# Tokens as the stationary side of the last product, and the last norm taken by partition

## The chip, the cores and the metric

One core of a Trainium2 chip runs the whole program. The metric is device time in microseconds (us), from the start of the program to its end. Engines are named as in the profile: PE is TensorE's matmuls and PEld its weight loads, DVE is VectorE, ACT is ScalarE, POOL is GpSimd, SP is SyncE, whose queue issues the loads of the weights.

## The reference, cut to what matters

```python
def rmsnorm(x, g):
    return x * lax.rsqrt(jnp.mean(x * x, axis=-1, keepdims=True) + EPS) * g

def swiglu(x, w_in, w_out):
    gate, up = jnp.split(x @ w_in, 2, axis=-1)
    return (jax.nn.silu(gate) * up) @ w_out

# h: (1, 512 tokens, 1024), D_FF = 2816, fp32
for i in range(2):                      # mixer A in layer 0, mixer B in layer 1
    h = h + 0.5 * swiglu(rmsnorm(h, norm_g[i, 0]), ffn_w_in[i, 0], ffn_w_out[i, 0])
    h = h + mixer(rmsnorm(h, norm_g[i, 1]))
    h = h + 0.5 * swiglu(rmsnorm(h, norm_g[i, 2]), ffn_w_in[i, 1], ffn_w_out[i, 1])
return rmsnorm(h, final_g)
```

The change concerns the end of the last line of the loop for i = 1 (the product with `ffn_w_out[1, 1]`) and the final `rmsnorm`.

## The kernel before

The residual h stays in SBUF as eight tiles `H[j]`, 128 features on the partitions by 512 tokens. Each fp32 factor is split into a high and a low part (`whi`, `wlo` for weights, `xh`, `xl` or `yh`, `yl` for activations) and a product is three matmuls in a row, L356 to L358: high by high, weights' high by low, weights' low by high. The weight block is the stationary side, the tokens move through the array.

`WeightStream` is the road of the weights. SP loads them in pieces of 128 by 1024 (`raw`, ring of 4 buffers), ACT copies a piece to `whi` (L173), DVE forms `wlo` (L176). A converted piece is a unit. Units of kind P hold eight 128 by 128 blocks; units of kind F are the seven forms of a two-level product with sums of weights (`two_pairs`), which runs the gate and up projections. Converted units live in a ring "w" of 3 pairs and, for F units alone, a ring "x" of 2 pairs. `PLAN` is the fixed order of all units. All engines run their instructions in the order in which the program issues them.

`ffn` ends in three chunks (`CHUNKS`): so many calls of `two_pairs`, which fill tiles `Y` with the gated activations, and then a product of these with the rows of `w_out`, added to H. In the last chunk of the last `ffn` the contraction is over 6 blocks of 128 (`n_k` = 6). Before the change this last product is run in two halves of 256 tokens (`parts` = 2), each with its own 6 units (the last `"P" * 6` of `PLAN` loads and converts the same weights again): first four output blocks side by side (`group`), then four one by one (`single`). After each output block DVE multiplies the bank by the token scale and adds it to H (L629, L630), ACT squares it (L306) and weighs it by the final gain (L1100), DVE adds up the squares (L307). At the end of a half, `norm_scale` sums the squares over the partitions by matmuls with a column of ones (L1109), takes a reciprocal root by Newton steps on DVE (`rsqrt`, L282 to L287), and `norm_rest` spreads the result over the partitions by a matmul (L1120) and multiplies all eight tiles by it: the first half's on POOL (L1128), during the second half's product, the second half's on DVE and POOL (L1126, L1128). The output is stored feature by token and turned on the host.

Of the kernel before, what the change touches and what calls it, by code (L numbers as in the profile page):

```python
# [12 lines left out]
F32 = mybir.dt.float32  # L13
# [6 lines left out]
P = 128  # L20
# [29 lines left out]
PLAN = FFN_PLAN + "P" * 37 + FFN_PLAN + FFN_PLAN + "P" * 72 + FFN_PLAN + "P" * 6  # L50
# [5 lines left out]
class WeightStream:  # L56
# [8 lines left out]
    def __init__(self, nc, pool, dram):  # L65
# [21 lines left out]
        self.lo_engine = nc.vector  # L87

# [142 lines left out]
def tile_trunk(ctx: ExitStack, tc, specs_out, xT, wst, gT, rel, onehot, bu, bv, lng, lnb, wspT, bsp, out):  # L231
# [167 lines left out]
    def ffn(layer, which, norm, finish, begin=None, hooks=None, parts=1, aside=None, mids={}):  # L399
# [10 lines left out]
        with tc.tile_pool(name=uname("ffn"), bufs=1) as fp:  # L410
# [17 lines left out]
            def temp(name):  # L428
                return fp.tile([P, S], F32, tag=name, bufs=1, name=uname(name))
# [163 lines left out]
            for ci, dps in enumerate(CHUNKS):  # L593
# [6 lines left out]
                for i in range(dps):  # L600
# [15 lines left out]

                end = ci == len(CHUNKS) - 1
                if end:
                    W.spool = None
                n = S // (parts if end else 1)  # L620
                for at in range(0, S, n):
                    s = slice(at, at + n)

                    def y_parts(k):
                        return Y[k // 2][0][:, k % 2, s], Y[k // 2][1][:, k % 2, s]

                    def add(j, ps):
                        t = gate_tile()[:, 0]
                        nc.vector.tensor_tensor(t[:, s], ps[:, s], R["h"][:, s], op=ALU.mult)  # L629
                        nc.vector.tensor_tensor(H[j][:, s], H[j][:, s], t[:, s], op=ALU.add)  # L630
                        if end:
                            finish(j, s)

                    first = [bank(tag0) for _ in range(4)]
                    group([ps[:, s] for ps in first], range(4), n_k, spec_out, y_parts,
                          hooks=mids if at else {})
                    for j in range(4):
                        add(j, first[j])
                    for j in range(4, KD):
                        ps = bank(tag1)  # L640
                        single(ps[:, s], j, n_k, spec_out, y_parts)
                        add(j, ps)
# [419 lines left out]
    def into(norm):  # L1062
        return lambda j, s: prepare(j, norm)
# [25 lines left out]
    parts = 2  # L1089
    nt = NT // parts  # L1090
    sq = []

    def finish(j, s):
        if j < KD - 1:
            square(j, s)
        else:
            if not sq:
                sq.append(small.tile([P, S], F32, tag="s1_512", bufs=1, name="last_sq"))
            nc.scalar.activation(sq[0][:, s], H[j][:, s], AF.Square)
        nc.scalar.activation(H[j][:, s], H[j][:, s], AF.Copy, scale=g_sb[:, 6, j:j + 1])  # L1100

    R = {}

    def norm_scale(s, end):
        sums = [bank("aux" if end else "acc") for _ in range(nt)]
        for part in (acc[0], sq[0]):
            for t in range(nt):
                at = s.start + t * P
                mm(sums[t][:, :1], part[:, at:at + P], ones[:, :1], start=part is not sq[0], stop=part is sq[0])  # L1109
        v = small.tile([P, nt], F32, tag="v", bufs=1, name=uname("v"))  # L1110
        for t in range(nt):
            nc.vector.tensor_scalar(v[:, t:t + 1], sums[t][:, :1], 1.0 / D, EPS, op0=ALU.mult, op1=ALU.add)
        R["c"] = rsqrt(v, [P, nt])

    def norm_rest(s, end):
        rc = R["c"]
        ps = bank("aux" if end else "acc")
        for t in range(nt):
            at = s.start + t * P
            mm(ps[:, at:at + P], rc[:, t:t + 1].broadcast_to([P, P]), ident, start=True, stop=True)  # L1120
        rb = small.tile([P, S], F32, tag="nwy512", bufs=1, name=uname("last_rb"))
        nc.scalar.activation(rb[:, s], ps[:, s], AF.Copy)
        for j in range(KD):
            o = H[j][:, s]
            if end and j not in (0, 3, 6):
                nc.vector.tensor_tensor(o, o, ps[:, s], op=ALU.mult)  # L1126
            else:
                nc.gpsimd.tensor_tensor(o, o, rb[:, s], op=ALU.mult)  # L1128
            queue = nc.gpsimd if not end else nc.sync if j % 2 else nc.scalar
# [58 lines left out]
```

## Time and profile before

| What | Value |
|---|---|
| Median of 3 runs | 2132.21 us (2132.17 to 2132.26) |
| Profiled execution, its own time | 2135.96 us |
| Its span (first to last instruction) | 2134.2 us |
| PE busy | 2089.1 us, 98% of the span |
| First matmul of the last product | starts at 2068.76 us |
| Last matmul of the last product | starts at 2120.83 us |

The span is 1.8 us shorter than the execution that it comes from. The profiled execution took 3.7 us more than the median of the timed runs, under 0.2%. Places in the program are given in us from the start of the span.

### The profile page before, as it was taken

The numbers are of one execution on the slowest core, as the hardware profiler recorded it, in microseconds if no ns is written. First come the engines' busy times: TensorE is split into PE (matmuls) and PEld (weight loads), VectorE is DVE, ScalarE is ACT, GpSimd is POOL, SyncE is SP. The second block draws the span as 40 slices with busy tenths as digits, with TensorE's granted clock in tenths as the row PEclk, the third lists the DMA queues.
The fourth block names the chain that finished last, engine by engine and source line by source line (L and its number), as shares of the span: only waits on it lengthen the run. The fifth ranks groups of instructions, "written<-read, shape, count | busy, mean of one in ns | idle before, by whom it ended". The sixth has DMA issues, their size and how long they took to land.

```text
span 2134.2 us, 29989 instructions
## 1 busy us (share of the span) xinstructions
PE 2089.1 (98%) x12344; PEld 1854.3 (87%) x12344; DVE 1500.7 (70%) x2052; ACT 899.3 (42%) x1163; POOL 91.2 (4%) x76
## 2 busy tenths in 40 slices
PE   8999999999999999999999999999999999999996
PEld 6989898788788899997989898788888888999895
DVE  6868687696758686776868686645845567687676
ACT  5535344334445344344535344333323245344353
POOL 0000000243200000000000000000000000000002
PEclk9999999999999999999999999999999999999997
DMA  4233332232122323222232322332232222223232
GB/s 170 96 115 112 105 125 82 89 104 85 60 89 89 119 96 102 100 99 79 99 107 97 113 90 95 134 100 88 84 101 92 82 97 99 99 99 102 96 118 70
DMA packets 59992, 212.34 MB, mean 99 GB/s; under 512 B 6904, under 2 KB 7992, under 8 KB 59728
## 3 DMA queue, kind: packets, MB, share of 16 engines
q1 hardware_dynamic: 56448, 201.35, 27.9%
q0 software_dynamic: 1680, 5.94, 0.8%
q10 hardware_dynamic: 1728, 3.15, 0.4%
q8 instruction: 96, 1.57, 0.3%
q14 instruction: 40, 0.33, 0.0%
HBM read 208.29 MB, written 4.74 MB: 100 GB/s over the span
## 4 chain that ended last, share of the span: by engine, by line
PE 81%; issue 8%; DVE 7%; ACT 3%; DMA 1%; POOL 0%; SPq 0%; POOLq 0%; ACTq 0%; DVEq 0%
PE acc L356 14%; PE acc L357 13%; PE acc L358 13%; PE aux L357 10%; PE aux L356 10%; PE aux L358 10%; DVE wlo L176 1%; ACT whi L173 1%; PE aux L967 1%; PE aux L969 1%; PE aux L968 1%; PE aux L1019 1%; PE acc L967 1%; PE acc L969 1%; PE acc L968 1%
## 5 line engine op out<-in xcount | busy, mean ns | idle before, releaser
L176 DVE TENSOR_TENSOR wlo<-raw,whi 128x1024 fp32r<-128x1024 f32 (+1 forms) x389 | 472.8, 1219 | 317.2 <-ACT whi L173 315.8
L173 ACT ACTIVATE whi<-raw 128x1024 fp32r<-128x1024 f32 (+1 forms) x416 | 433.4, 1050 | 483.1 <-PE acc L357 204.3
L356 PE MATMUL acc<-xh,whi 128*128 128x256 f32 (+1 forms) x888 | 306.6, 345 | 9.3 <-ACT xh L295 6.3
L357 PE MATMUL acc<-xl,whi 128*128 128x256 f32 (+1 forms) x888 | 296.8, 334 | 0.8 <-DVE xl L296 0.8
L358 PE MATMUL acc<-xh,wlo 128*128 128x256 f32 (+1 forms) x888 | 296.6, 334 | 0.0
L356 PEld LDWEIGHTS acc<-xh,whi 128*128 128x128 f32 x888 | 169.9, 191 | 28.3 <-ACT xh L295 6.7
L356 PE MATMUL aux<-xh,whi 128*128 128x256 f32 (+1 forms) x592 | 190.2, 321 | 1.2 <-ACT rh L396 1.2
L358 PE MATMUL aux<-xh,wlo 128*128 128x256 f32 (+1 forms) x592 | 190.0, 321 | 1.3 <-DVE wlo L176 1.3
L357 PE MATMUL aux<-xl,whi 128*128 128x256 f32 (+1 forms) x592 | 189.6, 320 | 0.0
L356 PE MATMUL acc<-th,whi 128*128 128x256 f32 x640 | 182.3, 285 | 6.0 <-ACT u L509 4.5
L357 PEld LDWEIGHTS acc<-xl,whi 128*128 128x128 f32 x888 | 170.0, 191 | 19.0 <-DVE xl L296 1.9
L358 PEld LDWEIGHTS acc<-xh,wlo 128*128 128x128 f32 x888 | 169.7, 191 | 16.9
L357 PE MATMUL acc<-tl,whi 128*128 128x256 f32 x640 | 182.0, 284 | 0.3 <-DVE tl L379 0.3
L358 PE MATMUL acc<-th,wlo 128*128 128x256 f32 x640 | 181.8, 284 | 0.0
L356 PE MATMUL acc<-yh,whi 128*128 128x512 f32 (+1 forms) x376 | 142.7, 379 | 5.1 <-ACT whi L173 5.1
L356 PE MATMUL aux<-th,whi 128*128 128x256 f32 x512 | 144.9, 283 | 0.0
L357 PE MATMUL aux<-tl,whi 128*128 128x256 f32 x512 | 144.9, 283 | 0.0
L358 PE MATMUL aux<-th,wlo 128*128 128x256 f32 x512 | 144.9, 283 | 0.0
L358 PE MATMUL acc<-yh,wlo 128*128 128x512 f32 (+1 forms) x376 | 142.5, 379 | 2.1 <-DVE wlo L176 2.1
L358 PE MATMUL aux<-yh,wlo 128*128 128x512 f32 (+1 forms) x376 | 142.1, 378 | 1.7 <-DVE wlo L176 1.5
L357 PE MATMUL acc<-yl,whi 128*128 128x512 f32 (+1 forms) x376 | 142.3, 379 | 0.0
L356 PE MATMUL aux<-yh,whi 128*128 128x512 f32 (+1 forms) x376 | 142.1, 378 | 0.0
(274 smaller groups left out, 4392.0 us busy)
## 6 DMA issues: line engine op xcount, KB each, us to landing
raw<-in_wst SPq DMA_DIRECT2D x378, 512.0 KB, 3.3
dist<-dist_rows ACTq DMA_DIRECT2D x8, 320.0 KB, 4.1
h<-in_xT SPq DMA_DIRECT2D x8, 256.0 KB, 7.2
tb<-dist POOLq DMA_DIRECT2D x8, 256.0 KB, 3.9
bias<-in_bv POOLq DMA_DIRECT2D x1, 1536.0 KB, 7.4
out<-h POOLq DMA_DIRECT2D x8, 128.0 KB, 2.0
raw<-in_wst SPq DMA_DIRECT2D x2, 256.0 KB, 3.9
wT<-in_wspT POOLq DMA_DIRECT2D x1, 512.0 KB, 8.9
```

The lines of the kernel that those rows point to most:

```text
L173: self.nc.scalar.activation(hi[:, s], src[:, s], AF.Copy)
L176: self.lo_engine.tensor_tensor(lo[:, s], src[:, s], hi[:, s].bitcast(F32), op=ALU.subtract)
L356: mm(ps, wh, xh, start=first, stop=False, **kw)
L357: mm(ps, wh, xl, start=False, stop=False, **kw)
L358: mm(ps, wl, xh, start=False, stop=last, **kw)
L967: mm(banks[t], xh, wh, start=k == 0, stop=False)
L968: mm(banks[t], xl, wh, start=False, stop=False)
L969: mm(banks[t], xh, wl, start=False, stop=k == KD - 1)
L1019: mm(ps[:, t * P:(t + 1) * P], V[t][:, d * P:(d + 1) * P], wT[:, g, :], start=True, stop=True)
```

## The change

The last product runs once, over all six units. The tokens become the stationary side (128 of them for each of four token tiles t) and the weights move, 512 columns (half of the 1024 output features) for each matmul. The result has tokens on the partitions and features along the row.

- `PLAN` loses its last six units; the last six (`LAST`) may use both rings and are all kept until the end. The sixth goes into `W.extra`, the tiles `TH[0]`, `TL[0]`, free once the last form has run.
- `turn_back` transposes the old residual on PE, four 128 by 128 blocks into one PSUM bank, and ACT copies the bank to a tile `final[t]`. There are eight of these: four stand between the forms of the last `two_pairs`, four between the steps k of the last product.
- The product runs over k with four banks open (t = 0, 1, two halves each), then bank by bank for t = 2 and 3, with the same kept weights.
- After a bank, `rest`: DVE multiplies it by the token's scale and adds the residual (one instruction, L1146), ACT squares it and sums along the row (`accum_out`, L1149), DVE multiplies by the gain (L1151), which is now a row, loaded by a DMA that repeats it on 128 partitions. After both halves of a token tile, `store`: `rsqrt` on one column, the scale of one half on ACT (L1163), of the other on DVE (L1161), and a store of 256 KB from each of the two queues ACT and SP.

The sums by matmul, the spreading matmul, POOL's multiplications and the second half's weights are gone.

```diff
-PLAN = FFN_PLAN + "P" * 37 + FFN_PLAN + FFN_PLAN + "P" * 72 + FFN_PLAN + "P" * 6
+PLAN = FFN_PLAN + "P" * 37 + FFN_PLAN + FFN_PLAN + "P" * 72 + FFN_PLAN
+LAST = 2 * CHUNKS[-1]
...
     def _parts(self, u, ring):
+        if ring is None:
+            self.conv[u] = self.extra
+            return self.extra
...
-            rings = [r for r in ("w", "x")[:1 if kind == "P" else 2] if self._free(r, self.current)]
+            kept = u >= len(self.units) - LAST
+            rings = [r for r in ("w", "x")[:1 if kind == "P" and not kept else 2]
+                     if self._free(r, len(self.units) - LAST if kept else self.current)
+                     and self._free(r, self.current)]
+            if kept and not rings and self.extra and u == len(self.units) - 1:
+                rings = [None]
...
+                    if last and n_dp == sum(CHUNKS) - 1:
+                        between = last[0](bank("acc"), gate_tile)
                     two_pairs(pair, "aux" if n_dp % 2 else "acc", between)
...
+                if end and last:
+                    W.extra = [x[0].rearrange("p a b -> p (a b)") for x in (TH, TL)]
+                    last[1](n_k, spec_out, y_parts, R["c"], temp)
+                    continue
...
-    ffn(1, 1, 5, finish, parts=parts, mids={2: lambda: norm_scale(head, False), 5: lambda: norm_rest(head, False)})
-    tail = slice(S - S // parts, S)
-    norm_scale(tail, True)
-    norm_rest(tail, True)
+    def turn_back(t, half):
+        ps = turned[0]
+        for i in range(4):
+            nc.tensor.transpose(ps[:, i * P:(i + 1) * P], H[4 * half + i][:, t * P:(t + 1) * P], ident)
+        if not half:
+            final[t] = W.spool.tile([P, D], F32, tag=("r22", "wsum")[t // 2], bufs=2, name=uname("turned"))
+        nc.scalar.activation(final[t][:, half * 512:(half + 1) * 512], ps, AF.Copy)
...
+        turn = [lambda a=a: turn_back(*a) for a in ((0, 0), (0, 1), (1, 1))]
+        return turn[:2] + [lambda: None] * 2 + [load_gains, turn[2]]
...
+        def product(t, half, ps, k):
+            if k not in weights:
+                weights[k] = W.take(*[spec(k, c) for c in range(KD)])
+            s = slice(half * 512, (half + 1) * 512)
+            wh, wl = (w[:, s] for w in weights[k])
+            yh, yl = y_parts(k, slice(t * P, (t + 1) * P))
+            mm(ps, yh, wh, start=k == 0, stop=False)
+            mm(ps, yl, wh, start=False, stop=False)
+            mm(ps, yh, wl, start=False, stop=k == n_k - 1)
...
+        def rest(t, half, ps):
+            x = final[t][:, half * 512:(half + 1) * 512]
+            nc.vector.scalar_tensor_tensor(x, ps, rh[:, t:t + 1], x, op0=ALU.mult, op1=ALU.add)
+            junk = small.tile([P, S], F32, tag="s0_512", bufs=1, name=uname("junk"))
+            i = 2 * t + half
+            nc.scalar.activation(junk, x, AF.Square, accum_out=sums[:, i:i + 1])
+            y = weighed[t, half] = temp(("m1", "m5", "u2", "u3")[i % 4])
+            nc.vector.tensor_tensor(y, x, gains[half], op=ALU.mult)
+
+        def store(t):
+            v = small.tile([P, 1], F32, tag="v", bufs=1, name=uname("v"))
+            nc.vector.tensor_tensor(v, sums[:, 2 * t:2 * t + 1], sums[:, 2 * t + 1:2 * t + 2], op=ALU.add)
+            nc.vector.tensor_scalar(v, v, 1.0 / D, EPS, op0=ALU.mult, op1=ALU.add)
+            rs = rsqrt(v, [P, 1])
+            for half, queue in ((0, nc.scalar), (1, nc.sync)):
+                y = weighed[t, half]
+                if half:
+                    nc.vector.tensor_scalar(y, y, rs[:, :1], None, op0=ALU.mult)
+                else:
+                    nc.scalar.activation(y, y, AF.Copy, scale=rs[:, :1])
+                queue.dma_start(out[t, :, half * 512:(half + 1) * 512], y)
+
+        group2 = [(t, half, bank("aux")) for t in range(2) for half in range(2)]
+        for k in range(n_k):
+            for t, half, ps in group2:
+                product(t, half, ps, k)
+            if k < 4:
+                turn_back(2 + k // 2, k % 2)
+        for t, half, ps in group2:
+            rest(t, half, ps)
+            if half:
+                store(t)
+        for t in range(2, NT):
+            for half in range(2):
+                ps = bank("acc")
+                for k in range(n_k):
+                    product(t, half, ps, k)
+                rest(t, half, ps)
+            store(t)
```

Three places show how the instructions now stand. The first is PE's queue where the last product begins, behind the last form of `two_pairs`. Before, the moving side stands ahead of the stationary one in a row: `yh`, `yl` move, 256 columns at a time.

```order
L358 MATMUL acc_17999<-th_15217,wlo_18063 128x256
L356 MATMUL aux_18225<-yh_17869,whi_18121 128x256
L357 MATMUL aux_18225<-yl_17870,whi_18121 128x256
L358 MATMUL aux_18225<-yh_17869,wlo_18122 128x256
L356 MATMUL aux_18226<-yh_17869,whi_18121 128x256
```

Now the same place of PE's queue reads as follows (the second to fourth bank's rows, of the same kind, lie between the two pieces):

```order
L1138 MATMUL aux_18259<-whi_18106,yh_17869 128x512
L1139 MATMUL aux_18259<-whi_18106,yl_17870 128x512
L1140 MATMUL aux_18259<-wlo_18107,yh_17869 128x512
...
L1108 MATMUL acc_17999<-ident,h_71 128x128
L1108 MATMUL acc_17999<-ident,h_72 128x128
L1108 MATMUL acc_17999<-ident,h_73 128x128
L1108 MATMUL acc_17999<-ident,h_74 128x128
L1138 MATMUL aux_18259<-whi_18139,yh_17869 128x512
```

The weights move, 512 columns at a time, and each step k uses one unit (`whi_18106`, then `whi_18139`), with four transposes of the residual behind it.

The second place is ACT's queue around the end of the last `two_pairs`: `whi` are conversions of units, L543 and L465 the silu and the high part of the last `Y`. Before:

```order
L173 ACTIVATE whi_18155<-raw_17995 128x1024
L173 ACTIVATE whi_18186<-raw_17997 128x1024
L543 ACTIVATE gate_18002<-gate_18002 128x1024
L465 ACTIVATE yh_18221<-gate_18002 128x1024
L173 ACTIVATE whi_18253<-raw_18033 128x1024
L173 ACTIVATE whi_18283<-raw_18125 128x1024
L303 ACTIVATE sqacc_18316<-h_71 128x256
```

Now (L553 and L475 are the same silu and high part, L1111 the copies of the turned residual):

```order
L183 ACTIVATE whi_18210<-raw_18034 128x1024
L1111 ACTIVATE turned_18184<-acc_17999 128x512
L183 ACTIVATE whi_18245<-raw_18110 128x1024
L553 ACTIVATE gate_18003<-gate_18003 128x1024
L475 ACTIVATE yh_18252<-gate_18003 128x1024
L1111 ACTIVATE turned_18279<-acc_17999 128x512
L183 ACTIVATE th_15214<-raw_18143 128x1024
L1111 ACTIVATE turned_18279<-acc_17999 128x512
L1111 ACTIVATE turned_18316<-acc_17999 128x512 x2
L1149 ACTIVATE junk_18360,last_sums_18258<-turned_18040 128x512
```

The fourth and fifth of the six units (`whi_18210`, `whi_18245`) have moved ahead of the silu, the sixth stands behind it, in `th_15214`, and no conversion is left behind it.

The third place is the end of DVE's queue. Before, after the last Newton step (`nwy`), it multiplies five tiles of the second half:

```order
L287 SCALAR_TENSOR_TENSOR nwy_18737<-nwt_18736,nwy_18737 128x2
L1126 TENSOR_TENSOR h_72<-h_72,aux_18749 128x256
L1126 TENSOR_TENSOR h_73<-h_73,aux_18749 128x256
L1126 TENSOR_TENSOR h_75<-h_75,aux_18749 128x256
L1126 TENSOR_TENSOR h_76<-h_76,aux_18749 128x256
L1126 TENSOR_TENSOR h_78<-h_78,aux_18749 128x256
```

Now this is all that DVE does for a token tile (t = 2), and then the first row of t = 3; the Newton steps between are 11 rows, of which the first and last stand:

```order
L1146 SCALAR_TENSOR_TENSOR turned_18279<-acc_18421,last_rh_18256,turned_18279 128x512
L1151 TENSOR_TENSOR m_1444_18443<-turned_18279,gate_18178 128x512
L1146 SCALAR_TENSOR_TENSOR turned_18279<-acc_18445,last_rh_18256,turned_18279 128x512
L1151 TENSOR_TENSOR m_1447_18467<-turned_18279,gate_18178 128x512
L1155 TENSOR_TENSOR v_18469<-last_sums_18258 128x1
L1156 TENSOR_SCALAR v_18469<-v_18469 128x1
L292 TENSOR_SCALAR nwi_18472<-v_18469 128x1
...
L297 SCALAR_TENSOR_TENSOR nwy_18474<-nwt_18473,nwy_18474 128x1
L1161 TENSOR_SCALAR m_1447_18467<-m_1447_18467,nwy_18474 128x512
L1146 SCALAR_TENSOR_TENSOR turned_18316<-acc_18490,last_rh_18256,turned_18316 128x512
```

The next tile's first instruction stands behind the whole chain of the tile before, on the same queue.

## Rows read from the trace of the kernel before

**Rows 1.** Windows: length, busy PE, PEld, DVE, ACT, POOL, clock, DMA share, GB/s.
```profile
2068.80:2083.60 14.80, 14.58 (x121) 14.37 (x120) 10.40 (x18) 7.99 (x13) 0.00 (x0) 1.00 0.34 108
2083.60:2098.40 14.80, 11.15 (x82) 9.96 (x81) 8.44 (x15) 7.67 (x13) 0.00 (x0) 1.00 0.31 107
2098.40:2109.40 11.00, 10.86 (x78) 10.43 (x77) 9.55 (x24) 4.12 (x9) 4.21 (x7) 0.84 0.07 24
2109.40:2121.30 11.90, 5.93 (x25) 5.27 (x24) 9.49 (x15) 4.93 (x10) 6.63 (x10) 0.61 0.18 66
2121.30:2134.20 12.90, 3.25 (x12) 2.78 (x12) 4.68 (x21) 1.41 (x4) 2.08 (x3) 0.50 0.25 81
```

**Rows 2.** Timeline of PE: start, duration, instruction (first two and last matmul).
```profile
2068.76 0.28 PE L356 MATMUL aux<-yh,whi 128*128 128x256 f32 x1
2068.88 0.28 PE L357 MATMUL aux<-yl,whi 128*128 128x256 f32 x1
...
2120.83 0.41 PE L358 MATMUL acc<-yh,wlo 128*128 128x256 f32 x1
```

**Rows 3.** PE's longest wait from 2068.8 to the end: total us, times, longest.
```profile
PE acc L356 <- ACT whi L173: 5.1, 2, 4.6
```

**Rows 4.** Timeline of DVE: one line while POOL multiplies, and later.
```profile
2105.94 1.19 DVE L307 TENSOR_TENSOR sqacc<-sqacc,sq 128x256 f32<-128x256 f32 x1 [0.48 <-ACT sq L306]
...
2120.89 0.42 DVE L307 TENSOR_TENSOR sqacc<-sqacc,sq 128x256 f32<-128x256 f32 x1 [0.48 <-ACT sq L306]
```

**Rows 5.** Timeline behind the last product: first and last instruction of the Newton steps.
```profile
2123.91 0.17 DVE L282 TENSOR_SCALAR nwi<-v 128x2 int32<-128x2 int32 x1
...
2125.88 0.16 DVE L287 SCALAR_TENSOR_TENSOR nwy<-nwt,nwy 128x2 f32<-128x2 f32 x1
```

**Rows 6.** Timeline of POOL: the two last multiplications.
```profile
2128.58 1.39 POOL L1128 TENSOR_TENSOR h<-h,last_rb 128x256 f32<-128x256 f32 x2
```

**Rows 7.** Timeline of PE, mixer B: weights moving, 512 columns (first and last of 22).
```profile
1360.94 0.39 PE L967 MATMUL aux<-whi,xh 128*128 128x512 f32 x1
...
1365.70 0.39 PE L967 MATMUL aux<-whi,xh 128*128 128x512 f32 x1
```

**Rows 8.** Timeline of PE at the program's start: 512 columns.
```profile
7.55 0.63 PE L356 MATMUL acc<-xh,whi 128*128 128x512 f32 x1
7.98 0.63 PE L357 MATMUL acc<-xl,whi 128*128 128x512 f32 x1
```

**Rows 9.** Timeline of PE in mixer A: four transposes, and the instruction behind them.
```profile
594.47 0.60 PE L874 MATMUL aux<-ident,pr 128*128 128x128 f32 x4
594.91 1.29 PE L886 MATMUL acc<-pT,v 128*128 128x128 f32 x7
```

**Rows 10.** One line's instructions: duration in ns, least, median, most.
```profile
L874 PE MATMUL aux<-ident,pr x80: 270/271/273, 500.8 to 594.8; 128*128 128x128 f32 x80
```

**Rows 11.** Groups by form: count, busy us, mean ns, idle before.
```profile
L984 DVE SCALAR_TENSOR_TENSOR z<-aux,rcol,bias 128x512 f32<-128x512 f32 x12 | 8.9, 739 | 3.9 <-PE aux L969 3.9
L542 DVE TENSOR_TENSOR gate<-gate,u 128x512 f32<-128x512 f32 x36 | 24.6, 685 | 0.0
L997 DVE TENSOR_SCALAR bv<-bv,mv,nwy 128x512 f32<-128x512 f32 x24 | 12.0, 542 | 0.0
L306 ACT ACTIVATE sq<-h 128x512 f32<-128x512 f32 x7 | 4.4, 623 | 3.3 <-DVE sqacc L307 3.3
L860 ACT ACTIVATION_READ_ACCUMULATOR pr<-lg,st 128x1 f32 x32 | 6.0, 187 | 0.0
L436 ACT ACTIVATE m<-h,g_sb 128x512 f32<-128x512 f32 x32 | 21.2, 710 | 0.0
```

**Rows 12.** Groups by form: the conversions of a unit.
```profile
L173 ACT ACTIVATE whi<-raw 128x1024 fp32r<-128x1024 f32 x412 | 431.2, 1054 | 483.1 <-PE acc L357 204.3 <-PE aux L357 138.2 <-issue 45.8
L176 DVE TENSOR_TENSOR wlo<-raw,whi 128x1024 fp32r<-128x1024 f32 x385 | 470.2, 1225 | 317.2 <-ACT whi L173 315.8
```

**Rows 13.** DMA issues: a row of DRAM repeated on 128 partitions, us to landing.
```profile
bias<-in_bv POOLq DMA_DIRECT2D x1, 1536.0 KB, 7.4
```

More of the change, by code (lines that the diff above doesn't have):

```diff
@@ L87, in __init__ @@
         self.lo_engine = nc.vector
+        self.extra = None
     def _free(self, ring, below):
@@ L230, in tile_trunk @@
 @with_exitstack
-def tile_trunk(ctx: ExitStack, tc, specs_out, xT, wst, gT, rel, onehot, bu, bv, lng, lnb, wspT, bsp, out):
+def tile_trunk(ctx: ExitStack, tc, specs_out, xT, wst, gT, gl, rel, onehot, bu, bv, lng, lnb, wspT, bsp, out):
     nc = tc.nc
@@ L397, in scale_rows, with ffn @@
         return rb, rh
-    def ffn(layer, which, norm, finish, begin=None, hooks=None, parts=1, aside=None, mids={}):
+    def ffn(layer, which, norm, finish, begin=None, hooks=None, aside=None, last=None):
         NJ = DFF // P
@@ L426, in ffn, with temp @@
                 begin(spare)
-            def temp(name):
-                return fp.tile([P, S], F32, tag=name, bufs=1, name=uname(name))
+            def temp(name, width=S):
+                return fp.tile([P, width], F32, tag=name, bufs=1, name=uname(name))
             def sums(kp):
@@ L615, in spec_out, with y_parts, add @@
                     return ("ffn_w_out", (layer, which), (p0 + k) * P, [(0, c * P, P)])
+                def y_parts(k, s=slice(0, S)):
+                    return Y[k // 2][0][:, k % 2, s], Y[k // 2][1][:, k % 2, s]
                 end = ci == len(CHUNKS) - 1
+                if end and last:
+                    W.extra = [x[0].rearrange("p a b -> p (a b)") for x in (TH, TL)]
+                    last[1](n_k, spec_out, y_parts, R["c"], temp)
+                    continue
                 if end:
                     W.spool = None
[L620 to L642, printed above, removed]
+                def add(j, ps):
+                    t = gate_tile()[:, 0]
+                    nc.vector.tensor_tensor(t, ps, R["h"], op=ALU.mult)
+                    nc.vector.tensor_tensor(H[j], H[j], t, op=ALU.add)
+                    if end:
+                        finish(j)
+                first = [bank(tag0) for _ in range(4)]
+                group(first, range(4), n_k, spec_out, y_parts)
+                for j in range(4):
+                    add(j, first[j])
+                for j in range(4, KD):
+                    ps = bank(tag1)
+                    single(ps, j, n_k, spec_out, y_parts)
+                    add(j, ps)
     def load_table(oh_sb):
@@ L1062, in into @@
     def into(norm):
-        return lambda j, s: prepare(j, norm)
+        return lambda j: prepare(j, norm)
     def behind(k):
@@ L1087, in tile_trunk @@
     mixer_b(5)
[L1089 to L1129, printed above, removed]
-            queue.dma_start(out[j, :, s], o)
@@ new lines, in tile_trunk, with last_block, load_gains, last_product @@
+    gains = []
+    def last_block(ps, tile):
+        turned[0] = ps
+        def load_gains():
+            t = tile()
+            nc.gpsimd.dma_start(t, bass.AP(tensor=gl.tensor, offset=gl.offset, ap=[[0, P], [1, D]]))
+            gains.extend(t[:, half] for half in range(2))
+            turn_back(1, 0)
+        turn = [lambda a=a: turn_back(*a) for a in ((0, 0), (0, 1), (1, 1))]
+        return turn[:2] + [lambda: None] * 2 + [load_gains, turn[2]]
+    def last_product(n_k, spec, y_parts, rc, temp):
+        rh = temp("last_rh", NT)
+        nc.vector.tensor_scalar(rh, rc, 0.5, None, op0=ALU.mult)
+        sums = temp("last_sums", 2 * NT)
+        weights = {}
+        def product(t, half, ps, k):
[7 more added lines that the diff above has]
+            mm(ps, yh, wl, start=False, stop=k == n_k - 1)
+        weighed = {}
+        def rest(t, half, ps):
[35 more added lines that the diff above has]
+            store(t)
@@ L1137, in tile_trunk @@
+    ffn(1, 1, 5, None, last=(last_block, last_product))
     assert len(W.specs) == N_PIECES
@@ L1175 @@
            for n, v in arrays.items()]
-    out = nc.dram_tensor("out_0", (KD, P, S), F32, kind="ExternalOutput").ap()
+    out = nc.dram_tensor("out_0", (NT, P, D), F32, kind="ExternalOutput").ap()
     specs = []
@@ L1186 @@
     got = r.results[0]["out_0"]
-    return c(got.reshape(D, S).T).reshape(1, S, D)
+    return c(got.reshape(1, S, D))
```

3 lines of the change are left out of this document (2 added, 1 removed).

## The prediction

> **What bounds the kernel now.** I read the windows of the last product first, then PE's timeline there, then the waits, then the chain behind the last matmul. Up to the last product the order of the instructions stays as it is, but for four transposes with their copies and two conversions that move, so only what lies behind 2068.76 [rows 2] can pay.
>
> The last product runs from 2068.76, and its last matmul starts at 2120.83 [rows 2]; the span ends at 2134.2 [rows 1]. So 52.1 us go to the product and 13.4 us to what follows. The product is 2 halves x 8 output blocks x 6 steps x 3 = 288 matmuls of 256 columns. They start 0.12 us apart [rows 2], which makes 34.6 us. The other 17.5 us are waits and slow stretches. The windows show where: 3.7 us of 14.8 without a matmul in the second, 6.0 of 11.9 in the fourth, and a granted clock of 0.84, then 0.61, then 0.50 of full speed [rows 1], the mean of stretches at 2.4 and at 1.2 GHz. The reader is to see that PE waits here for ACT and DVE, once for 4.6 us for a `whi` [rows 3]. These engines alternate between the old output blocks' additions, squares and gains and the second half's conversions, and while POOL multiplies the first half an addition on DVE takes 1.19 us instead of 0.42 [rows 4]. Behind the product the chain is serial: sums, Newton steps of 2.13 us (2123.91 to 2125.88 + 0.16) [rows 5], spreading, multiplying until 2129.97 (2128.58 + 1.39) [rows 6], then 4.2 us of stores up to 2134.2.
>
> **The change, part by part, as new places in the span.**
>
> *The matmuls.* 144 of 512 columns with the weights moving. Mixer B has the same form: 21 steps from 1360.94 to 1365.70, 0.2267 us each [rows 7]. So 144 x 0.2267 = 32.6 us, only 2 us under the old 34.6; the gain is not in the arithmetic. Per unit PE now works 12 x 0.2267 = 2.72 us, while a conversion takes 1.05 on ACT and 1.23 on DVE [rows 12]: the converters are faster than PE.
>
> *The transposes.* 8 x 4. Mixer A's four transposes are followed 0.44 us later by the next instruction [rows 9]. They stand between other small matmuls there; I take 0.5 us for four, since a change between streams can cost a weight load that is not covered. The bounds are 0.44 and, if each waited for the one before, 4 x 0.27 = 1.08 [rows 10]. I stay near the first, which is the distance itself where the second is a duration. Eight make 4.0 us (3.5 to 8.7): 2.0 ahead of the product, 2.0 within it. The Trainium skill, "TensorE: Matmul & The Clock Gate", Part 4, speaks against this part: it gives a transpose in PE's transpose mode some 275 ns in a kernel. The rows' 271 ns duration agrees with that, their distance of 0.11 us does not. By the page's figure taken as a distance the eight would cost 8.8 us.
>
> *The first four banks.* They begin at 2068.76 + 2.0 = 2070.8, take 72 x 0.2267 = 16.3 and 2.0 of transposes, and end at G = 2089.1. Nothing waits, I think. The sixth unit can be converted only when the last form is done at 2070.8. Behind that lie on ACT and DVE, at most one after the other: the fifth unit's `whi` 1.05, the silu (as wide) 1.05, two multiplications 2 x 0.69, the high part 1.05, one copy of a turned bank 0.62, the sixth `whi` 1.05 and `wlo` 1.23 [rows 11, 12], together 7.4 us, with the low part of `Y` beside it at most 8.7. It is needed at step k = 5, 5 x 2.72 + 2.0 = 15.6 us after the start. If that cover of 7 us were gone, PE would wait for the rest. The gain's row comes by a DMA from POOL's queue, issued before the last two forms have run and needed only behind G, over 18 us later; 1536 KB of the same kind landed in 7.4 us [rows 13], so its 512 KB are hidden.
>
> *The work behind the banks.* For each token tile DVE does, by rows: two additions of the residual 2 x 0.74, two multiplications by the gain 2 x 0.69, two instructions on a column 2 x 0.17 and the Newton steps 2.13 [rows 5], and a scale of half a tile 0.54 [rows 11]: 5.9 us. The sum of squares on ACT, 0.62 + 0.19 [rows 11], runs beside the second multiplication by the gain and lasts 0.12 longer; with some 0.15 us of gaps it is 6.15 us, gaps and columns being the part that I estimate. Tiles 0 and 1 come at once at G. Their first bank is ready when 9 of the group's matmuls are left, so DVE begins at G - 1.9. Three tiles take 18.4, up to G + 16.5, and the fourth 2 x 0.74 + 0.69 + 0.81 + 0.35 + 2.13 + 0.71 (ACT's scale of the other half) and gaps, 6.3: G + 22.8. PE ends sooner: 72 x 0.2267 = 16.3, and from G + 16.5 (the last result) a free DVE would need the same without the first half's 0.74 + 0.69, to G + 21.4. Since DVE only begins tile 3 when its last bank is ready, I take the later: DVE ends last, at G + 22.8 = 2111.9. No other instruction on DVE waits behind it, POOL has none, so the 1.19 us of [rows 4] doesn't come back.
>
> *The stores.* Before, the last multiplication ends 4.2 us ahead of the end [rows 1, 6], with four stores of 128 KB on each of two queues. Now the last are one of 256 KB on each, the same bytes as two of the old in each queue. I keep 4.2 (3.5 to 5). The earlier tiles' stores lie beside matmuls. Their buffers are used again two tiles later, 12 us by DVE's count: hidden.
>
> *What goes without a price of its own:* six loads of 512 KB and six conversions; the stalls that they fed are in the old 52.1 us. Four copies on ACT (0.62 each) and two conversions that now stand earlier, in the last `two_pairs`: PE takes 7 x 24 matmuls x 0.12 = 20 us for its seven forms, in which nine conversions, the silu, the high part and the four copies take ACT 11 x 1.05 + 4 x 0.62 = 14 us; if the cover failed, it would cost up to the copies' 2.5.
>
> *Sum:* 2068.8 + 2.0 + 16.3 + 2.0 + 22.8 + 4.2 = 2116.1 against 2134.2, 18.1 us less. I take the difference off the median, since the profiled execution (2135.96, with the span in it) lies 3.75 us above that: 2132.2 - 18.1 = **2114.1 us**, 0.85% faster. About 0.2%, 4.3 us, is what a measurement can tell from no change.
>
> **The rivals.**
>
> *PE and not DVE ends last.* If DVE's instructions overlap as unrelated ones can, the end is G + 21.4: 2112.7. For it: the sums above differ by 1.4 us only. Against: `store` for a tile stands whole ahead of the next tile on one queue.
>
> *The transposes are dear.* At 0.27 us each: 8.7 - 4.0 = 4.7 us more, 2118.8. For it: their duration [rows 10]. Against: the distance [rows 9]. By the Trainium skill's page on TensorE, Part 4, it would be 8.8 - 4.0 more, 2118.9; the trace agrees with its duration and so far not with that as a distance.
>
> *A wait stays in the first four banks.* A unit or a turned bank comes late, once or twice: each costs one conversion, 1.05 + 1.23 = 2.3 us [rows 12], and where the clock falls as in the third window (11.0 us at 0.84, so 3.5 us of it at half speed [rows 1]), 8 matmuls at 0.43 us [rows 8] instead of 0.23, 1.6 us: 2118.0 for one to 2121.9 for two. For it: the six units now depend on five pairs of buffers and one that the last form frees. Against: the cover of 7 us.
>
> *The clock stays at 1.2 GHz through the product (slower).* A matmul of 512 columns at that level starts 0.43 us after the last [rows 8]. For all 144 it is 144 x (0.43 - 0.2267) = 29.3 us more: 2143.4. It decides from (18.1 + 4.3) / 0.203 = 110 matmuls on. For it: in the old product the clock fell after waits [rows 1], and 32 small transposes now lie in the stream. Against: in the first window the clock is 1.00 with PE busy, and the new stream has no wait that I find. From 68 slow matmuls on, the change would not be told from none.
>
> *The change doesn't remove the stall.* Were the waits of ACT and DVE due to the squares and additions alone, they would return as DVE's 24 us; but these lie behind matmuls, not ahead of them, and only the last tile's shows. It would need 14 us of new waits to be "same".
>
> **How the numbers follow.** My forecast, DVE last within 1.5 us, 45 in 100; PE last or shorter stores (2110.5 to 2112.7) 20; dear transposes 10; a wait 17; between 2128 and 2136.5 by several waits or half of the product at low clock 5; slower by the clock 3. The range leaves out the last two groups and the far end of the wait: low is all lower bounds together (transposes -0.5, PE last -1.4, stores -0.7) and 1.0 for the gaps that I put in by hand, 2110.5; high is the wait of 2.3 and 1.6 us twice, 2122. Faster 0.92, same 0.05, slower 0.03.
>
> **What would show it.** Right: starts of the 512-column matmuls 0.227 us apart up to the end, clock near 1.00 until then, no wait of PE over 0.3 us; the first matmul of the product near 2070.8 and the last near 2105; the last Newton step near 2111.2, DVE without idle time from about 2087. Wrong: a wait of PE for `th`, `tl` or `turned`, four transposes over 0.6 us, a step of 0.43 us, or a store chain behind the last scale over 5 us.

## The result, and the profile after

The changed kernel takes 2112.5 us (median of 4 runs, 2112.1 to 2113.0) beside 2132.2 us for the kernel before on the same chip: a ratio of 0.9903, 95% interval 0.9891 to 0.9915, 19.7 us less. The profiled execution took 2112.86 us, 0.36 above that median, with a span of 2110.8.

Windows of the changed kernel: the first four banks, the other four, and what lies behind PE (columns as in [rows 1]).

```profile
2067.00:2085.20 18.20, 18.20 (x90) 15.08 (x89) 7.66 (x10) 7.03 (x10) 0.00 (x0) 1.00 0.00 1
2085.20:2101.70 16.50, 16.50 (x73) 13.33 (x72) 14.60 (x53) 5.80 (x13) 0.00 (x0) 1.00 0.17 64
2101.70:2110.80 9.10, 0.02 (x1) 0.00 (x0) 4.73 (x18) 2.17 (x5) 0.00 (x0) 0.63 0.31 115
```

PE is busy in every microsecond of the product, at a granted clock of 1.00, and no wait of PE is recorded from 2040 to the end, where [rows 1] had stretches without a matmul and [rows 3] waits. What stood behind the last matmul has shrunk from 13.4 to 9.5 us.

Timeline of PE: the product's first matmuls, the first four transposes in it, the fifth bank's first matmul, and the last of all (beside [rows 2, 9]).

```profile
2066.99 0.40 PE L1138 MATMUL aux<-whi,yh 128*128 128x512 f32 x1
2067.22 0.40 PE L1139 MATMUL aux<-whi,yl 128*128 128x512 f32 x1
...
2069.51 0.39 PE L1140 MATMUL aux<-wlo,yh 128*128 128x512 f32 x1
2069.74 0.60 PE L1108 MATMUL acc<-ident,h 128*128 128x128 f32 x4
2070.10 0.48 PE L1138 MATMUL aux<-whi,yh 128*128 128x512 f32 x1
2070.41 0.40 PE L1139 MATMUL aux<-whi,yl 128*128 128x512 f32 x1
...
2085.24 0.39 PE L1138 MATMUL acc<-whi,yh 128*128 128x512 f32 x1
...
2101.33 0.39 PE L1140 MATMUL acc<-tl,yh 128*128 128x512 f32 x1
```

Matmuls start 0.227 us apart. Four transposes put 0.36 us between their first and the next matmul, and the step behind that is 0.31 instead of 0.227: 0.45 us in all.

Timeline of DVE and ACT at the end: the last of token tile 2 and the course of tile 3. Three dots stand for rows left out, most of them Newton steps.

```profile
2100.70 0.49 DVE L1161 TENSOR_SCALAR m<-m,nwy 128x512 f32<-128x512 f32 x1
2101.10 0.75 DVE L1146 SCALAR_TENSOR_TENSOR turned<-acc,last_rh,turned 128x512 f32<-128x512 f32 x1
2101.88 0.69 DVE L1151 TENSOR_TENSOR u<-turned,gate 128x512 f32<-128x512 f32 x1
...
2102.49 0.74 DVE L1146 SCALAR_TENSOR_TENSOR turned<-acc,last_rh,turned 128x512 f32<-128x512 f32 x1
2103.27 0.69 DVE L1151 TENSOR_TENSOR u<-turned,gate 128x512 f32<-128x512 f32 x1
2103.33 0.63 ACT L1149 ACTIVATE junk<-turned 128x512 f32<-128x512 f32 x1 [0.72 <-DVE turned L1146]
2103.87 0.19 ACT L1149 ACTIVATION_READ_ACCUMULATOR junk<-turned 128x1 f32 x1
2104.09 0.16 DVE L1155 TENSOR_TENSOR v<-last_sums 128x1 f32<-128x1 f32 x1
...
2104.47 0.15 DVE L292 TENSOR_SCALAR nwi<-v 128x1 int32<-128x1 int32 x1
...
2106.39 0.16 DVE L297 SCALAR_TENSOR_TENSOR nwy<-nwt,nwy 128x1 f32<-128x1 f32 x1
2106.59 0.72 ACT L1163 ACTIVATE u<-u,nwy 128x512 f32<-128x512 f32 x1 [2.54 <-DVE nwy L297]
```

The last matmul ends at 2101.72, and DVE takes its bank only at 2102.49, since tile 3 stands behind all of tile 2 on its queue. From 2107.31 the two stores take 3.5 us.

### The profile page after: what moved, and what is told of

The parts are those of the page before. It is cut to its first block, busy times and chain, and to the rows that moved or that the text cites. A ratio compares the mean times of both kernels' runs of the same rounds, so it can differ in the third digit from the quotient of the medians.

```text
span 2110.8 us, 29664 instructions
## 1 busy us (share of the span) xinstructions
PE 2076.8 (98%) x12208; PEld 1839.1 (87%) x12208; DVE 1487.5 (70%) x2044; ACT 891.3 (42%) x1151; POOL 78.8 (4%) x58
## 4 chain that ended last, share of the span: by engine, by line
PE 88%; DVE 7%; ACT 3%; issue 2%; DMA 0%; ACTq 0%; DVEq 0%; POOLq 0%
PE acc L366 15%; PE acc L367 15%; PE acc L368 15%; PE aux L366 10%; PE aux L367 10%; PE aux L368 10%; DVE wlo L186 1%; ACT whi L183 1%; PE aux L979 1%; PE aux L980 1%; PE aux L981 1%; PE aux L1031 1%; PE acc L979 1%; PE acc L980 1%; PE acc L981 1%
## 5 line engine op out<-in xcount | busy, mean ns | idle before, releaser
L186 DVE TENSOR_TENSOR wlo<-raw,whi 128x1024 fp32r<-128x1024 f32 (+1 forms) x382 | 464.2, 1219 | 309.7 <-ACT whi L183 308.2
L183 ACT ACTIVATE whi<-raw 128x1024 fp32r<-128x1024 f32 (+1 forms) x409 | 426.5, 1050 | 485.1 <-PE acc L367 203.7
L366 PEld LDWEIGHTS acc<-th,whi 128*128 128x128 f32 x640 | 122.8, 192 | 8.5 <-ACT u L519 6.8
L366 PE MATMUL acc<-yh,whi 128*128 128x512 f32 x328 | 127.7, 389 | 0.0
L367 PE MATMUL acc<-yl,whi 128*128 128x512 f32 x328 | 127.7, 389 | 0.0
L366 PE MATMUL aux<-yh,whi 128*128 128x512 f32 x328 | 127.6, 389 | 0.0
L367 PE MATMUL aux<-yl,whi 128*128 128x512 f32 x328 | 127.6, 389 | 0.0
```

What stands on the lines that cost most here:

```text
L183: self.nc.scalar.activation(hi[:, s], src[:, s], AF.Copy)
L186: self.lo_engine.tensor_tensor(lo[:, s], src[:, s], hi[:, s].bitcast(F32), op=ALU.subtract)
L366: mm(ps, wh, xh, start=first, stop=False, **kw)
L367: mm(ps, wh, xl, start=False, stop=False, **kw)
```

## The experiments

All times are medians, and each ratio is to runs of the kernel before on the same chip (2132.2 to 2133.2 us). The runs fall into three groups: where the 19.7 us came from, the terms of the sum, and a loss that two of the edits brought with them.

**One pass alone, first try.** The kernel before, with its last product run once over 512 tokens, weights still stationary; the last norm is one tail.

```diff
-PLAN = ... + FFN_PLAN + "P" * 6
+PLAN = ... + FFN_PLAN
...
-    parts = 2
+    parts = 1
...
-    ffn(1, 1, 5, finish, parts=parts, mids={2: ..., 5: ...})
+    ffn(1, 1, 5, finish, parts=parts)
```

> The kernel before with its last product in one pass over all 512 tokens: weights stationary as before, the six units loaded and converted once, the whole norm taken behind the product. If the gain is the end of the stalls that the second set of conversions fed, the product needs 144 x 0.227 = 32.6 us with under 2 us of waits instead of 52.1, and the chain behind it grows from 13.4 us to 17 or 18, since additions, multiplications and stores are twice as wide: about 14 us less than before, 2118. If the gain is the turned orientation with the norm by partition, the waits stay with the old additions and squares, and the time lies within 3 us of 2132.

Measured: 2133.2 us, ratio 1.0005 (0.9995 to 1.0014). The expectation failed, though its mechanism was there: PE waited no longer for a `whi` or a `wlo`. The loss lay elsewhere, and PE's groups by form show it, the first row in this kernel, the second in the kernel before:

```profile
L356 PE MATMUL aux<-yh,whi 128*128 128x512 f32 x352 | 139.6, 396 | 0.0
...
L356 PE MATMUL aux<-yh,whi 128*128 128x512 f32 x328 | 127.6, 389 | 0.0
```

These 512-column matmuls take 389 ns in the changed kernel too. All but 24 of the 352 belong to second products of the four feed-forward layers that the edit doesn't touch. It does touch one thing that lies under them: with one norm over four columns instead of two over two, three tiles of 32 bytes in the pool `small` are gone, and everything allocated behind that pool lies 96 bytes lower in SBUF.

**One pass alone, in its place.** The same with `pad(small, 128)` instead of 32.

> The kernel before with one pass of the last product, old orientation (weights stationary, 512 tokens moving), units of chunks 4 and 5 read once, and 96 bytes of pad that give the small tiles the size they have in the kernel before. Theory that the lost time was the stalls of the two halves: with y matmuls at 389 ns again the earlier 2133.2 falls by some 14 to 17 us, to 2116 to 2120 (the last norm still stands as one tail of 17 us behind the product). Rival, that the time of the change comes from its orientation and one pass is worth nothing by itself: 2131 to 2133.

Measured: 2119.4 us, ratio 0.9939 (0.9917 to 0.9960), and 389 ns again. So running the product once is worth 13.7 of the 19.7 us, with the old orientation and the old norm (by the interval of the ratio, 8.5 to 17.7). It takes away two things together: the second preparation of the units, and POOL's multiplication beside a second half. The next three runs take them away, one at a time and then together. Windows of this kernel, the product and what follows:

```profile
2070.00:2104.00 34.00, 33.67 (x153) 27.68 (x151) 20.99 (x28) 13.30 (x18) 0.00 (x0) 1.00 0.02 8
2104.00:2123.50 19.50, 4.99 (x24) 4.52 (x24) 7.49 (x23) 3.26 (x5) 3.71 (x3) 0.59 0.29 108
```

The product has no wait, as in the changed kernel. But its last matmul starts at 2103.28, and 19.8 us follow its end, where the changed kernel has 9.1: all four token tiles' norm lies behind the last matmul. That is 10.7 us, of which the transposes take 3.6 back (below); the times differ by 6.9.

**Units kept, halves as before.** The old halves, with the second half using the first half's converted units.

```diff
-PLAN = ... + FFN_PLAN + "P" * 6
+PLAN = ... + FFN_PLAN
...
+again = iter(list(pieces))
+W.take = (lambda *sp: next(again)) if at else (lambda *sp: pieces.append(take(*sp)) or pieces[-1])
```

> The kernel before, two halves of 256 tokens, weights stationary, norm as before, but with the change's stream of weights: the six units are converted once, kept in five pairs of buffers and the freed tiles, and used again by the second half. If the stalls came from the second set of conversions, PE's waits for whi and wlo in the second half (4.6 and 1.3 us) and the low clock behind them go, and those of the first half shrink because five pairs are filled ahead: about 15 us less than before, 2117. If they came from the additions and squares of the old orientation, the time stays over 2128.

Measured: 2123.1 us, ratio 0.9949 (0.9929 to 0.9968), 6 us short. The waits for `whi` and `wlo` are gone. A new one is there, in PE's waits of this kernel:

```profile
PE aux L1125 <- DVE sqacc L317: 7.1, 1, 7.1
```

It lies behind the product, as PE's timeline shows with the last matmul and the first sum of squares:

```profile
2104.99 0.28 PE L368 MATMUL acc<-yh,tl 128*128 128x256 f32 x1
2112.37 1.01 PE L1125 MATMUL aux<-ones,sqacc 128*128 128x1 f32 x4 [7.10 <-DVE sqacc L317]
```

The product itself has no stall left: from its first matmul (2068.77) to its last it takes 36.2 us, where the kernel before took 52.1. But DVE is late at its end. On the timelines of DVE and POOL stand an addition of two SBUF tiles (L643) ahead of POOL's multiplications, an instruction that reads PSUM (L642) beside one of them, and an addition beside another:

```profile
2086.83 0.42 DVE L643 TENSOR_TENSOR h<-h,gate 128x256 f32<-128x256 f32 x1
...
2098.59 0.42 DVE L642 TENSOR_TENSOR gate<-aux,rh 128x256 f32<-128x256 f32 x1
2098.79 0.75 POOL L1144 TENSOR_TENSOR h<-h,last_rb 128x256 f32<-128x256 f32 x1
...
2101.86 1.28 DVE L643 TENSOR_TENSOR h<-h,gate 128x256 f32<-128x256 f32 x1
2102.10 0.76 POOL L1144 TENSOR_TENSOR h<-h,last_rb 128x256 f32<-128x256 f32 x1
```

Beside POOL's multiplications DVE's additions of two SBUF tiles take three times as long and end behind POOL's instruction (2103.14 and 2102.86); the one instruction with an input from PSUM that runs beside one keeps its 0.42 us. The Trainium skill, "SBUF — State Buffer", section "SBUF: two separate sides", names such a pair: a DVE instruction with two SBUF inputs and a GpSimd instruction that reads SBUF take turns on one port pair. These rows agree.

**No multiplication on POOL.** The kernel before without POOL's multiplication of the first half, which so leaves without its token scale.

```diff
-            else:
+            elif end:
                 nc.gpsimd.tensor_tensor(o, o, rb[:, s], op=ALU.mult)
```

> The kernel before without POOL's eight multiplications of the first half: that half of the output is stored without its token scale. If DVE's slowing beside POOL (1.19 us for 0.42) is what made the 4.6 us wait for the whi, DVE's instructions of the second half take 0.42 us again, the wait falls under 2 us, and 4 to 8 us go: 2124 to 2128. If the wait comes from the order of the conversion behind the squares alone, under 2 us go.

Measured: 2127.7 us, ratio 0.9982 (0.9971 to 0.9994): 4.6 us, and the longest wait for a `whi` falls from 4.6 [rows 3] to 1.7.

**Both.** Kept units and no multiplication of the first half on POOL.

> The halves of the kernel before with the weight units kept between them, and without GpSimd's multiplication of the first half of the output by its token scale (that half leaves without it). Theory of two causes (units prepared twice, and VectorE's additions three times as long beside GpSimd's multiplication): the wait of 7.1 us for the square sums that was left with kept units goes, and the time is 2114.5 to 2118.5, the sum of the two gains or better. Rival, one cause (the wait for squares has nothing to do with GpSimd): 2122 to 2123, as with kept units alone.

Measured: 2118.7 us, ratio 0.9931 (0.9912 to 0.9950). The two gains, 9.2 and 4.6 us, add up to 13.8, and this run gives 14.3. PE's wait in it, and the last matmul of its product:

```profile
PE aux L1125 <- DVE sqacc L317: 2.0, 1, 2.0
...
2100.63 0.28 PE L368 MATMUL acc<-yh,tl 128*128 128x256 f32 x1
```

So two things cost time in the kernel before, units prepared twice and DVE held up by POOL, and the change takes away both. They don't cost it in the same place. The product's stall needs the units prepared twice: with kept units it takes 36.2 us with POOL's multiplications and without them (2064.41 to 2100.63). With units prepared twice, dropping POOL's multiplications shortens it from 52.1 to 45.9 us (2064.41 to 2110.34 in the run before this one). With kept units, what POOL costs stands behind the product: from the last matmul's start to the end 20.4 us with its multiplications and 14.7 without. From the product's first matmul to the end, which leaves out what the clock did ahead of it, the profiles give 65.4 us for the kernel before, 61.2 without POOL's multiplications, 56.6 with kept units, 50.9 with both edits, 52.7 with one pass in its place and 43.8 for the changed kernel.

**Every transpose twice.** The changed kernel, with `for i in 2 * list(range(4))` in `turn_back`.

> The changed kernel with each of the 32 transposes done twice, the second over the first. If four transposes cost their distance in the stream, about 0.45 us, the eight groups add 3.6 us: 2116.1. If they cost their duration of 0.27 us each, they add 8.7 us: 2121.2. The doubled ones carry no change of stream, so the first figure may come out nearer 3 us.

Measured: 2117.9 us (2115.4 to 2122.1), ratio 0.9928 (0.9907 to 0.9948), which alone doesn't choose. The trace does. Timeline of PE in this kernel, at the place shown above:

```profile
2077.04 0.39 PE L1140 MATMUL aux<-wlo,yh 128*128 128x512 f32 x1
2077.27 1.03 PE L1108 MATMUL acc<-ident,h 128*128 128x128 f32 x8
2078.06 0.48 PE L1138 MATMUL aux<-whi,yh 128*128 128x512 f32 x1
```

Eight take 0.79 us up to the next matmul where four took 0.36, 0.11 us for each added one. From the product's first matmul to its last it is 36.06 us instead of 34.34, 16 transposes more for 1.72. So the transposes of the changed kernel cost 32 x 0.107 us and their fixed parts: 1.9 us within the product (34.34 less 143 x 0.2267), and 1.7 ahead of it, 3.6 in all. The 1.7 are read from the way between the first matmul of the last chunk and the first of the product: 62.18 us in the changed kernel (2004.81 to 2066.99) and 60.48 in the kernel before (2008.28 to 2068.76). With 3.6 us more the time would be 2116.1, the lower of the two expectations; the median is 1.8 us above it, within this run's interval.

**The gain on POOL.** For tiles 0 to 2.

```diff
-            nc.vector.tensor_tensor(y, x, gains[half], op=ALU.mult)
+            (nc.vector if t == NT - 1 else nc.gpsimd).tensor_tensor(y, x, gains[half], op=ALU.mult)
```

> The changed kernel with the multiplication by the gain on POOL for the token tiles 0 to 2, which takes 6 x 0.69 us from DVE's queue. If DVE is only relieved, 0.7 us go as with one root. If POOL's reading slows DVE as it did in the kernel before (1.19 us for 0.42), DVE's additions and Newton steps stretch, its queue falls behind, and the time stays or grows by up to 3 us.

Measured: 2113.8 us, ratio 0.9907 (0.9891 to 0.9924): not told from the changed kernel. From the product's first matmul to the end it is 44.8 us instead of 43.8. DVE gives away 1.38 us a tile and is not earlier for it: its tiles lie 6.2 us apart (5.9 before this edit). An addition of two columns on DVE's timeline, and the wait ahead of it, show why; the two rows ahead of it are DVE's additions from PSUM and POOL's multiplications:

```profile
2083.60 1.43 DVE L1146 SCALAR_TENSOR_TENSOR turned<-aux,last_rh,turned 128x512 f32<-128x512 f32 x2 [8.96 <-PE aux L1140]
2084.44 2.55 POOL L1151 TENSOR_TENSOR m<-turned,gate 128x512 f32<-128x512 f32 x2 [21.33 <-DVE turned L1146]
2085.90 1.10 DVE L1155 TENSOR_TENSOR v<-last_sums 128x1 f32<-128x1 f32 x1 [0.87 <-ACT junk L1149]
```

One element for each partition, 0.16 us above and 1.10 here, beside POOL's multiplications of two SBUF tiles: it ends at 2087.00, POOL's two at 2086.99. The 0.87 us ahead of it are a wait for ACT's sum of squares, which DVE's own gain multiplication had covered to 0.13. Together they make 1.7 us, more than the 1.38 given away. The second addition from PSUM (L1146) runs beside POOL too and is not longer: 1.43 us for the two, 0.75 us for one in the changed kernel.

**One chain of Newton steps for tiles 0 and 1, first try.**

```diff
-        for t, half, ps in group2:
-            rest(t, half, ps)
-            if half:
-                store(t)
+        for t, half, ps in group2:
+            rest(t, half, ps)
+        store(0, 2)
```

> The changed kernel with one chain of Newton steps for the token tiles 0 and 1 together, which takes about 2.5 us from DVE's queue. If DVE's queue is what ends last, its first instruction on the last bank follows the last matmul at once (in the changed kernel it starts 0.77 us after that matmul's end) and 0.7 us go, 2111.8. If PE's last matmul sets the end already, nothing moves.

Measured: 2124.3 us, ratio 0.9954 (0.9939 to 0.9968), 12 us the wrong way. Here too the time was lost long before the edit: the product's first matmul starts at 2079.03 instead of 2066.99, and the 512-column groups on `yh` and `yl` take 395 ns. The columns of two widths made four more tiles of 32 bytes in `small`, so what lies behind had moved 128 bytes up. That became the next experiment.

**Only the place.** The changed kernel with `pad(small, 160)` instead of 32, and no instruction changed.

> The changed kernel with one edit: the pad of 32 bytes ahead of the small tiles is 160 bytes, which is what the extra small tiles of the kernel with one root for two token tiles added; no instruction differs. That kernel and the one-pass kernel both lost time in stages long before the last product, where their 512-column matmuls on the y tiles took 395 and 396 ns in place of 389. Theory of placement (small tiles move the tiles that lie behind them in SBUF, and the moving side is read more slowly): those matmuls at 395 ns again and the time at 2123 to 2126 us. Rival, that the instructions of those two edits did it: 2112.5 and 389 ns.

Measured: 2124.5 us, ratio 0.9955 (0.9942 to 0.9969). Groups of PE by form in this kernel:

```profile
L366 PE MATMUL acc<-yh,whi 128*128 128x512 f32 x328 | 129.5, 395 | 0.0
L366 PE MATMUL acc<-byh,whi 128*128 128x512 f32 x160 | 63.4, 396 | 0.0
```

128 bytes of padding cost 12 us, 0.6%. The rival, that the joined chain did it, is out.

**One chain, in its place.** The joined chain with the small tiles at their old size and number.

> The changed kernel with one chain of Newton steps for token tiles 0 and 1, and the small tiles kept at the size and the place they have in the changed kernel. Theory of placement: y matmuls at 389 ns, VectorE early at the last token tile instead of 0.8 us late, so 2111.8 us (2111.2 to 2112.3). Rival, that joining the chains itself costs what the first try of it showed: 2124. Rival, that the last 0.8 us of VectorE is no part of the end: 2112.5.

Measured: 2113.7 us (2111.2 to 2116.3), ratio 0.9906 (0.9887 to 0.9926), too wide to choose. By the profile the stretch from the product's first matmul (2067.55) to the end (2110.7) is 43.1 us instead of 43.8, and DVE takes the last bank 0.04 us after its matmul's end instead of 0.77, by these rows of PE and DVE:

```profile
2101.89 0.39 PE L1141 MATMUL acc<-tl,yh 128*128 128x512 f32 x1
2102.32 0.75 DVE L1147 SCALAR_TENSOR_TENSOR turned<-acc,last_rh,turned 128x512 f32<-128x512 f32 x1
```

So the 0.7 us are there, and are too small for these times.

**Another place for `th` and `tl`.** The changed kernel with these tiles 96 bytes lower and the others where they were.

```diff
-            pad(fp, 352 if begin else 448)
+            pad(fp, 256 if begin else 352)
...
+            pad(fp, 96)
             spare = y_tiles()
```

> The changed kernel with the th and tl tiles of each feed-forward layer 96 bytes lower in SBUF and everything else in its place (96 bytes of pad taken from ahead of them and put behind them). In the one-pass kernel whose small tiles were 96 bytes shorter, the 256-column matmuls on th and tl took 281 to 283 ns instead of 283 to 284, while those on the y tiles rose from 389 to 396. Theory that it is the place of the tile that a matmul reads as its moving side: th groups of bank aux at 281 ns, y groups at 389, and by the summed busy time of those six groups 3 to 4.5 us less, 2108 to 2109.5. Rival, that the 2 ns belong to something else in that kernel: 2112.5.

Measured: 2104.1 us (2103.2 to 2105.2), ratio 0.9860 (0.9843 to 0.9877): 8 us faster than the changed kernel, more than expected. A group of PE on `th` and one on the y tiles here, and the first of them in the changed kernel:

```profile
L366 PE MATMUL aux<-th,whi 128*128 128x256 f32 x512 | 143.4, 280 | 0.0
L366 PE MATMUL acc<-yh,whi 128*128 128x512 f32 x328 | 127.6, 389 | 0.0
...
L366 PE MATMUL aux<-th,whi 128*128 128x256 f32 x512 | 144.9, 283 | 0.0
```

The summed durations of the six groups of 256-column matmuls on `th` and `tl`, 3456 in all, are 8.6 us less than in the changed kernel, twice what the one-pass kernel had let expect, and the product's first matmul starts at 2059.33, 7.7 us earlier. The intervals of the two ratios lie apart.

**Both together.**

> The same move of th and tl together with the one chain of Newton steps for token tiles 0 and 1 (small tiles in their place), which took 0.7 us off the stretch from the last product's first matmul to the end in the profile of that kernel, but could not be told from the changed kernel in its times. If both hold: 2107.5 to 2109, and 43.1 us from the product's first matmul to the end. If the place of th does nothing: 2111.8.

Measured: 2105.0 us (2104.1 to 2107.1), ratio 0.9867 (0.9852 to 0.9882), and 43.3 us from the product's first matmul (2059.38) to the end (2102.7), where the kernel with `th` moved alone has 43.9. The time lies below the 2107.5 expected, as in the run before it. It is not told from the kernel with `th` moved alone; either beats both kernels of this study.

## Why the prediction was right

The forecast was 2114.1 us, with 2110.5 to 2122.0 as its range; 2112.5 was measured, and the mechanism was the forecast one: DVE, not PE, ends last.

- *The start* (2070.8) was off by 3.8 us: 2066.99. This is no gain of the change: 3.5 of the 3.8 us are there already at the first matmul of the last chunk (2008.28 before, 2004.81 after), ahead of every instruction that the change adds, and the other 0.3 are transposes at 1.7 us instead of 2.0. The clock records of the two traces put 17.1 us at half speed ahead of the product in the profile before and 6.8 us in the one after; the kernel before without POOL's multiplication, with 6.8 too, starts that chunk at 2003.94. The lead didn't reach the forecast, since the difference was taken off the median: the profiled execution lay 3.75 us above it before and 0.36 after.
- *The first four banks* were to take 18.3 us, and took 18.25 (2066.99 to 2085.24). 0.2267 us a matmul from mixer B [rows 7] was measured as 0.227, and four transposes at 0.45 to 0.48 us where 0.5 was taken; the dear rival is out by its doubled transposes. No wait and no fall of the clock came.
- *DVE* was to begin at G - 1.9 (measured G - 1.84) and take 6.15 us a tile. It took 5.90, the bare sum of its instructions by the rows (5.87). The gap for ACT's sum of squares is there (0.13 us, 2103.96 to 2104.09), but DVE starts the instruction behind a gain multiplication 0.08 us ahead of that one's end, so that no gap is left over the tile. The last scale ended at G + 22.1, forecast G + 22.8. The rival that PE ends last lies at 2112.7, next to the result, and still is not what happened, as the 0.77 us between the last matmul's end and DVE's use of its bank show. With the chains of two tiles joined it does happen, and gives 0.7 us. One reason that the prediction gives is wrong: DVE does not begin tile 3 only when its last bank is ready, but takes the tile's first bank at 2101.10, 0.62 us before the last matmul ends.
- *The stores* were to take 4.2 us and took 3.5, the lower bound: one store on each queue is not four.

From the product's first matmul to the end the forecast had 45.3 us and the profile has 43.8. With these 1.5 us the forecast difference of 18.1 becomes 19.6, and 19.7 was measured: DVE's gaps (0.7) and the stores (0.7) were the terms too large.

What the prediction had not divided was the stall: it counted 17.5 us of waits and slow clock as gone with the second half's conversions. The experiments split it: the product's own stall needs the units prepared twice, and POOL's hold on DVE adds to it and to the tail. The kernel with one pass and the old orientation already has 13.7 of the 19.7 us, and the orientation gives the other 6 or 7 by a shorter tail, not by a faster product.

## What to carry to other kernels

Where a product runs twice for the sake of an early tail, look at what the second run prepares again: running it once was worth more here than the overlap that the halves bought, and turning the result so that each token tile can finish by itself gave the overlap back. Before an experiment's time is read, compare the durations of instructions that the edit doesn't touch; a changed tile size elsewhere may have moved the operands of thousands of matmuls. Reading a difference from a landmark near the edit (here the product's first matmul) resolves 0.7 us where whole times can't.

## What the runs showed of the hardware

- **The place of a tile in SBUF changes the pace of the matmuls that stream it.** 512-column matmuls on the y tiles: a duration of 389 ns in the kernels before and after, 396 with the tiles 96 bytes lower and 395 with them 128 bytes higher. In these runs all that lies behind the pool moved with them. It is a matter of pace: the one-pass product takes 33.5 us from first to last matmul 96 bytes lower (2078.84 to 2112.33) and 32.4 in its place (2070.84 to 2103.28). 256-column matmuls on `th` and `tl`: 283 ns, 280 with these tiles alone 96 bytes lower, and 282 where all that lies behind the pool is 128 bytes higher, the place in which the y tiles' matmuls are slow. With 128 bytes up for all that lies behind the pool, the whole kernel takes 12 us more; with 96 down for `th` and `tl`, 8 less; no instruction differs. Which property of the address counts was not found: only these offsets were run.
- **A DVE instruction with two SBUF inputs waits out POOL's multiplication of two SBUF tiles, even one of a single column**: 0.16 became 1.10 us for one column, 0.42 became 1.28 for 256, and 0.42 stayed for 256 with one input from PSUM.
- **A further transpose beside others in a stream of 512-column matmuls takes 0.107 us**, though each row shows some 271 ns of duration [rows 10].
